# Gate and value projections of five feed-forward layers by seven products of block sums instead of eight, with the residual stream kept in DRAM between norms

## The chip, the cores and the metric

One core of a Trainium2 chip runs the whole network: two layers of a first block and one second block, 512 tokens of 1024 features, one launch. The metric is device time in microseconds. Names of the engines in the profile: PE is TensorE (matrix products), PEld its weight loads, DVE is VectorE, ACT is ScalarE, POOL is GpSimd, SP is SyncE, whose queue issues most DMAs. PSUM holds the results of TensorE in eight banks of 128x512 fp32; everything else lies in SBUF.

## The reference, cut to what matters

All arithmetic is fp32. The feed-forward layer occurs five times, twice in each layer of the first block and once in the second:

```python
D_MODEL, SEQ, D_FF = 1024, 512, 2816
def swiglu(x, w1, w3, w2):
    return (jax.nn.silu(x @ w1) * (x @ w3)) @ w2

for l in range(2):                                   # first block
    x = layer_norm(a * x + 0.5 * swiglu(x, ffn1...), ...)
    x = layer_norm(a * x + hybrid_mixer(x, ...), ...)
    x = layer_norm(a * x + 0.5 * swiglu(x, ffn2...), ...)
...                                                  # second block: recurrences, then
x = x + swiglu(rms_norm(x), ...)                     # its feed-forward, and a last rms_norm
```

## The kernel before, in words

**Exact products.** Activations lie feature-major: block k of 128 features is a tile of 128 partitions by 512 tokens (X0 to X7 for the residual stream). TensorE is fed with fp32r, a shortened fp32, so each operand is split in two: hi is the fp32r cast (ScalarE), lo is the operand minus hi (VectorE or POOL). One product is then three matrix products, hi with hi, hi with lo, lo with hi (`mm3`). In the trace x3h and x3l are the two parts of activation block 3, wraw a weight tile of 128x1024 as loaded, whi and wlo its parts (four buffers each; wraw has three), h0h to h21l the parts of the hidden blocks, kwh and kwl weight parts that are kept in slots.

**A feed-forward (`ffn`, line 714).** For each of 22 hidden blocks of 128 features the gate and the value are 8 blocks of x times a weight tile of 128x1024: 24 products of 512 columns in one PSUM bank (tile pu). ScalarE casts whi and applies SiLU to the gate (tile sl), VectorE makes wlo, multiplies by the value (sl<-sl,pu) and makes the low part of the hidden block; POOL has nothing to do there. The first three of the 44 banks are made together by `gemm_head`, 256 tokens at a time (72 products of 256 columns for each half), so that work can start while the norm before it is still on its second half. Then the down projection (`blocks`, tile po) makes 8 output blocks from 22 hidden blocks, the last two a half of the tokens at a time, and `layer_norm` adds each to X.

**A norm.** The last blocks of a projection come half by half, so the first half of the tokens is normed while TensorE makes the second. Statistics go through TensorE (sums, rbc: scale and offset spread to all partitions in PSUM), a chain of tiny VectorE operations (lnst), and then for each block VectorE multiplies and adds rbc, ScalarE writes the hi part, POOL the lo part.

**Order.** Each engine works through one fixed list. The lists are made when the kernel is recorded and do not always keep the order in which the code issues the work. Matrix weights are loaded by the SP queue in the order of use. All instructions pass through one wrapper, so that every row of the trace has the line L204; tiles and shapes tell them apart.

**Names that the steps touch:** `ffn` 714, `up` 710, `gemm_head` 459, `blocks` 444, `kept` 479, `wload` 395, `split` 409, `layer_norm` 592, `apply_norm` 649, `rms_end` 677, `start` and `first` at the end.

## Time and profile before

| | |
|---|---|
| three runs | 3388.19, 3385.47, 3387.38 us, median 3387.38 us |
| the profiled execution | span 3383.5 us from the first to the last instruction; the page gives no other time of its own, and the runs lie 2.0 to 4.7 us above it |
| granted TensorE clock, mean | 0.988 of full speed |
| busy | PE 97%, PEld 82%, DVE 51%, ACT 37%, POOL 17% |
| HBM | 274.76 MB read, 8.39 MB written, 84 GB/s over the span |

The chain of waits lies on TensorE for most of the span, and a good third of the span is the tile pu, the up-projections of the five feed-forwards. On POOL, 571.5 us are spread over the mixers, the norms and the second block. A matrix product's recorded duration is longer than the time to the next one's start, since they are pipelined: the pace is read from starts.

### The profile page before, as it was taken

How to read it: one execution, taken by the hardware profiler on the slowest of the kernel's cores; microseconds unless marked ns; L12 is line 12 of the kernel's file. 1: busy time of each engine (PE TensorE's matmuls, PEld its weight loads, DVE VectorE, ACT ScalarE, POOL GpSimd, SP SyncE). 2: the span in 40 equal slices, each digit the busy share in tenths (PEclk: the TensorE clock that was granted, in tenths of full speed). 3: DMA queues.
4: the chain of work that ended last, by engine and by line, in shares of the span. 5: the costliest groups of instructions: out<-in, count | busy, mean ns of one | idle time of the engine just before them, and what ended most of it. 6: DMA issues, size and time to landing. Idle time of an engine off the chain costs nothing.

```text
span 3383.5 us, 43373 instructions
## 1 busy us (share of the span) xinstructions
PE 3291.7 (97%) x17206; PEld 2759.6 (82%) x17210; DVE 1710.0 (51%) x3300; ACT 1242.4 (37%) x2224; POOL 571.5 (17%) x415
## 2 busy tenths in 40 slices
PE   9999999999999999999999999999999999999998
PEld 7888887788888888888778888888876777898887
DVE  4333668673333533366867433555526666443332
ACT  3232343543222422234354422335624444232221
POOL 0001430030002200044002100224442221030001
PEclk9999999999999999999899999989999999999999
DMA  4223211013233222322101223313341112423232
GB/s 157 97 93 108 63 58 57 7 51 100 95 94 105 82 95 97 98 72 70 57 7 51 85 96 96 109 56 104 116 130 64 61 65 88 145 88 100 94 97 72
DMA packets 88508, 285.96 MB, mean 85 GB/s; under 512 B 9840, under 2 KB 13552, under 8 KB 88304
## 3 DMA queue, kind: packets, MB, share of 16 engines
q1 hardware_dynamic: 83696, 275.84, 25.4%
q10 hardware_dynamic: 4608, 7.34, 0.7%
q8 instruction: 135, 2.21, 0.3%
q14 instruction: 69, 0.57, 0.1%
HBM read 274.76 MB, written 8.39 MB: 84 GB/s over the span
## 4 chain that ended last, share of the span: by engine, by line
PE 83%; DVE 9%; issue 3%; ACT 2%; POOL 2%; DMA 0%; SPq 0%; POOLq 0%; DVEq 0%; ACTq 0%
PE pu L204 35%; PE po L204 18%; PE sc L204 3%; PE pos L204 3%; PE pz L204 2%; PE pw L204 2%; PE so L204 2%; PE plx L204 2%; PE sz L204 2%; PE pgate L204 2%; PE pol L204 2%; POOL wlo L204 1%; PE ply L204 1%; PE pxb L204 1%; DVE isc L204 1%
## 5 line engine op out<-in xcount | busy, mean ns | idle before, releaser
L204 ACT CAST whi<-wraw 128x1024 fp32r<-128x1024 f32 (+7 forms) x507 | 507.9, 1003 | 1443.1 <-issue 486.0
L204 DVE TENSOR_TENSOR wlo<-wraw,whi 128x1024 fp32r<-128x1024 f32 (+1 forms) x326 | 394.0, 1209 | 613.9 <-ACT whi L204 598.9
L204 POOL TENSOR_TENSOR wlo<-wraw,whi 128x1024 fp32r<-128x1024 f32 (+6 forms) x181 | 394.1, 2181 | 630.4 <-ACT whi L204 622.7
L204 POOL TENSOR_TENSOR kwl<-wraw,kwh 128x512 fp32r<-128x512 f32 (+1 forms) x48 | 67.3, 1423 | 1694.6 <-ACT kwh L204 1677.2
L204 DVE TENSOR_TENSOR sl<-sl,pu 128x512 f32<-128x512 f32 x110 | 75.7, 688 | 343.8 <-PE pu L204 341.0
L204 PE MATMUL pu<-x0h,whi 128*128 128x512 f32 (+1 forms) x235 | 88.1, 379 | 7.1 <-ACT whi L204 7.1
L204 DVE SCALAR_TENSOR_TENSOR X<-X,po 128x512 f32<-128x512 f32 (+1 forms) x40 | 23.2, 580 | 138.8 <-PE po L204 138.8
L204 PE MATMUL pu<-x3l,whi 128*128 128x512 f32 (+1 forms) x235 | 88.4, 377 | 1.1 <-POOL x3l L204 1.1
L204 PE MATMUL pu<-x0l,whi 128*128 128x512 f32 (+1 forms) x235 | 88.6, 378 | 0.9 <-POOL x0l L204 0.9
L204 PE MATMUL pu<-x0h,wlo 128*128 128x512 f32 (+1 forms) x235 | 88.7, 378 | 0.6 <-DVE wlo L204 0.6
L204 PE MATMUL pu<-x1h,wlo 128*128 128x512 f32 (+1 forms) x235 | 88.7, 378 | 0.0
L204 PE MATMUL pu<-x2l,whi 128*128 128x512 f32 (+1 forms) x235 | 88.7, 378 | 0.0
L204 PE MATMUL pu<-x6l,whi 128*128 128x512 f32 (+1 forms) x235 | 88.2, 376 | 0.4 <-POOL x6l L204 0.4
L204 PE MATMUL pu<-x1l,whi 128*128 128x512 f32 (+1 forms) x235 | 88.6, 377 | 0.0
L204 PE MATMUL pu<-x4l,whi 128*128 128x512 f32 (+1 forms) x235 | 88.1, 376 | 0.4 <-POOL x4l L204 0.4
L204 PE MATMUL pu<-x5l,whi 128*128 128x512 f32 (+1 forms) x235 | 88.2, 376 | 0.2 <-POOL x5l L204 0.2
L204 ACT ACTIVATE sp<-sc,st 128x384 f32<-128x384 f32 (+3 forms) x128 | 66.6, 527 | 59.3 <-DVE st L204 47.0
L204 PE MATMUL pu<-x2h,wlo 128*128 128x512 f32 (+1 forms) x235 | 88.3, 377 | 0.0
L204 PE MATMUL pu<-x1h,whi 128*128 128x512 f32 (+1 forms) x235 | 88.3, 377 | 0.0
L204 PE MATMUL pu<-x3h,wlo 128*128 128x512 f32 (+1 forms) x235 | 88.3, 376 | 0.0
L204 PE MATMUL pu<-x7h,whi 128*128 128x512 f32 (+1 forms) x235 | 88.2, 375 | 0.0
L204 PE MATMUL pu<-x7l,whi 128*128 128x512 f32 (+1 forms) x235 | 88.2, 375 | 0.0
(1628 smaller groups left out, 9589.7 us busy)
## 6 DMA issues: line engine op xcount, KB each, us to landing
wraw<-in_ffn_in_dram SPq DMA_DIRECT2D x220, 512.0 KB, 3.8
wraw<-in_ffn_out_dram SPq DMA_DIRECT2D x80, 512.0 KB, 3.6
wraw<-in_ffn_out_dram SPq DMA_DIRECT2D x40, 384.0 KB, 3.1
wraw<-in_w_xbc_dram SPq DMA_DIRECT2D x24, 512.0 KB, 3.2
wraw<-in_wout_dram SPq DMA_DIRECT2D x16, 512.0 KB, 3.3
wraw<-in_w_gate_dram SPq DMA_DIRECT2D x16, 512.0 KB, 3.2
wraw<-in_w_z_dram SPq DMA_DIRECT2D x16, 512.0 KB, 3.2
wraw<-in_w_ossm_dram SPq DMA_DIRECT2D x16, 512.0 KB, 3.7
```

Of the source, the lines that this page charges most:

```text
L204: return f(*[_plain(x) for x in args], **{k: _plain(x) for k, x in kw.items()})
```

## The change

The hidden features are taken in 11 units of 256. A unit's gate and value weights are four quarters of 128x1024: a and b are the gate's for features 0 to 511 and 512 to 1023 of x, c and d the value's. x has four quarters as well, halves of the features by halves of the tokens. Seven products of sums of quarters replace the eight products of quarters (Strassen's form, in Winograd's arrangement); each is 24 matrix products of 256 columns, and results are added up in PSUM and by VectorE.

- `Unit` does a unit: it loads a, b, c, d (0.5 MB each, the same bytes as before), makes the sums s = c + d, s - a and b - (s - a) on VectorE and a - c on POOL, splits each of the seven weights (hi on ScalarE; lo on VectorE for products 1, 6 and 3, on POOL for 2, 5, 7 and 4), and puts the outputs together (su1, su5, su6 copied by ScalarE, three additions and four half multiplications on VectorE).
- `quarter_sums` makes t5, t6 (VectorE) and t7, t4 (POOL), sums of quarters of x, and splits them, once for each feed-forward, when the second half of the tokens has been normed.
- Hidden blocks (tiles hr) stay unsplit and are split later (hdh, hdl), by turns on VectorE and POOL, most of them during the last unit.
- To make room the residual stream is stored to DRAM after each norm (`spill`, SP's queue) and fetched again before the next down or output projection (`refill`, ScalarE's queue). 67 slots instead of 73; six wraw buffers instead of three. `blocks` keeps 16 of the 22 weight blocks of its first tail block and loads the other six for each half.

An up-projection was 984 matrix products of 512 columns and 144 of 256; it is now 1848 of 256 (11 units of 7 by 24). POOL's list grows from 420 to 782 rows.

```diff
-        for j in range(22):
-            pg, pu = (first.pop(0) if first else self.gemm(w, xs, "pu") for w in self.up(i, j))
-            s = self.a("sl")
-            nc.scalar.activation(s, pg, AF.Silu)
-            nc.vector.tensor_tensor(s, s, pu, op=OP.mult)
-            hid.append(self.split(s, f"h{j}"))
+        n = 11
+        plan = [(0, 1), (0, 2), (1, 1), (1, 2)] + [(0, p) for p in (5, 6, 3, 7)] + [(1, 5), (0, 4)] + [(1, p) for p in (6, 3, 7)]
+        for u in range(2, n):
+            plan += [(u, 1), (u, 5), (u, 2), (u - 1, 4), (u, 6), (u, 3), (u, 7)]
+        plan.append((n - 1, 4))
+        self.join_banks()
+        for u, p in plan:
+            if u not in units:
+                units[u] = Unit(self, io["ffn_in"][i, u], u < 2)
+            hidden = units[u].product(p, ops[p])
...
+            while raw and len(self.slots) > 8 + 2 * len(units) + 2 * (n - 1 - u):
+                hid.append(self.split(raw.pop(0), "hd", (nc.vector, nc.gpsimd)[len(hid) % 2]))
+        while raw:
+            hid.append(self.split(raw.pop(0), "hd", (nc.vector, nc.gpsimd)[len(hid) % 2]))
+        self.part_banks()
+        self.refill(x, home)
         yield from self.blocks([io["ffn_out"][i, m] for m in range(KD)], hid, "po", 2)

+class Unit:
+    def halves(self, raw, lower):
+        hi = net.wp.tile([P, WCH], F32R, name="whi", tag="whi", bufs=4)
+        lo = net.wp.tile([P, WCH], F32R, name="wlo", tag="wlo", bufs=4)
+        net.nc.scalar.copy(hi, raw)
+        lower.tensor_tensor(lo, raw, hi.bitcast(F32), op=OP.subtract)
...
+        if p == 5:
+            s = raw["s"] = net.wp.tile([P, WCH], F32, name="wraw", tag="wraw", bufs=6)
+            c, d, a = (self.load(q) for q in "cda")
+            dve.tensor_tensor(s, c, d, op=OP.add)
+            w = self.halves(s, pool)
+            pool.tensor_tensor(c, a, c, op=OP.subtract)
+            dve.tensor_tensor(s, s, a, op=OP.subtract)
+            return w
+        if p == 6:
+            return self.halves(raw["s"], dve)
+        if p == 3:
+            b = self.load("b")
+            dve.tensor_tensor(b, b, raw["s"], op=OP.subtract)
+            return self.halves(b, dve)
+        return self.halves(raw["c" if p == 7 else "d"], pool)
...
+        for f in range(2):
+            for k, (x, c) in enumerate(xs):
+                w = slice((4 * f + k) * P, (4 * f + k + 1) * P)
+                for j, (l, r) in enumerate(((hi, x[0]), (hi, x[1]), (lo, x[0]))):
+                    nc.tensor.matmul(bank[:, HALVES[f]], l[:, w], r[:, c], ...)
+        if p in (1, 5, 6):
+            s = sums[p] = net.a(f"su{p}")
+            nc.scalar.copy(s, bank)
+        elif p in (2, 3):
+            s = sums[{2: 1, 3: 6}[p]]
+            tt(s, bank, s, op=OP.add)
+            nc.scalar.activation(s, s, AF.Silu)
+        elif p == 7:
+            tt(sums[5], bank, sums[5], op=OP.add)
+            self.out = [net.a("hr") for _ in range(2)]
+            for o, h in zip(self.out, HALVES):
+                tt(o[:, HALVES[1]], sums[6][:, h], sums[5][:, h], op=OP.mult)
+        else:
+            for o, h in zip(self.out, HALVES):
+                tt(o[:, HALVES[0]], sums[1][:, h], bank[:, h], op=OP.mult)

+    def quarter_sums(self, ys, i, ops):
...
+            dve.tensor_tensor(t[5], a2, a1, op=OP.subtract)
+            dve.tensor_tensor(t[6], b2, t[5], op=OP.subtract)
+            pool.tensor_tensor(t[7], b2, a2, op=OP.subtract)
+            pool.tensor_tensor(t[4], b1, t[6], op=OP.subtract)
+        for n, lower in ((5, dve), (6, dve), (7, pool), (4, pool)):
+            q = self.split(ts.pop(n), f"t{n}", lower)
```

**VectorE, in the middle of an up-projection** (names: wlo, sl, h2l as above; su1, su5, su6 partial results, hr the unsplit hidden block, the numbers are buffers). Before, for one hidden block and the next:

```order
L204 TENSOR_TENSOR wlo<-wraw,whi 128x1024
L204 TENSOR_TENSOR h2l<-sl,h2h 128x512
L204 TENSOR_TENSOR wlo<-wraw,whi 128x1024
L204 TENSOR_TENSOR sl<-sl,pu 128x512
L204 TENSOR_TENSOR wlo<-wraw,whi 128x1024
L204 TENSOR_TENSOR h3l<-sl,h3h 128x512
```

and now, for one unit of two hidden blocks:

```order
L214 TENSOR_TENSOR wlo_1691<-wraw_1588,whi_1690 128x1024
L214 TENSOR_TENSOR wlo_1722<-wraw_1627,whi_1721 128x1024
L214 TENSOR_TENSOR wraw_1817<-wraw_1818,wraw_1820 128x1024
L214 TENSOR_TENSOR su1_1586<-pu_1633,su1_1586 128x512
L214 TENSOR_TENSOR hr_1551<-su1_1357,pu_1332 128x256
L214 TENSOR_TENSOR hr_1552<-su1_1357,pu_1332 128x256
L214 TENSOR_TENSOR wlo_1787<-wraw_1784,whi_1786 128x1024
L214 TENSOR_TENSOR wraw_1817<-wraw_1817,wraw_1784 128x1024
L214 TENSOR_TENSOR su6_1718<-pu_1600,su6_1718 128x512
L214 TENSOR_TENSOR wraw_1856<-wraw_1856,wraw_1817 128x1024
L214 TENSOR_TENSOR su5_1625<-pu_1561,su5_1625 128x512
L214 TENSOR_TENSOR hr_1780<-su6_1718,su5_1625 128x256
```

Three sums of weight tiles (wraw on both sides of the arrow) have joined three low parts (wlo); one half multiplication more, the second hr of products 7, follows.

**POOL, at the head of the second feed-forward, after the mixer's norm.** Before, the low parts of the first half of the tokens are followed by those of the second:

```order
L204 TENSOR_TENSOR x4l_6559<-X4_108,x4h_6558 128x256
L204 TENSOR_TENSOR x5l_6561<-X5_120,x5h_6560 128x256
L204 TENSOR_TENSOR x6l_6563<-X6_126,x6h_6562 128x256
L204 TENSOR_TENSOR x7l_6565<-X7_132,x7h_6564 128x256
L204 TENSOR_TENSOR x0l_6551<-X0_72,x0h_6550 128x256
```

and now:

```order
L214 TENSOR_TENSOR x4l_7683<-X4_7181,x4h_7682 128x256
L214 TENSOR_TENSOR wlo_7968<-wraw_7959,whi_7967 128x1024
L214 TENSOR_TENSOR x5l_7685<-X5_7183,x5h_7684 128x256
L214 TENSOR_TENSOR x7l_7689<-X7_7187,x7h_7688 128x256
L214 TENSOR_TENSOR x6l_7687<-X6_7185,x6h_7686 128x256
L214 TENSOR_TENSOR x4l_7683<-X4_7181,x4h_7682 128x256
L214 TENSOR_TENSOR t7_7748<-X4_7181,X0_7173 128x256
L214 TENSOR_TENSOR t4_7749<-X4_7181,t6_7747 128x256
L214 TENSOR_TENSOR x5l_7685<-X5_7183,x5h_7684 128x256
L214 TENSOR_TENSOR t7_7748<-X5_7183,X1_7175 128x256
L214 TENSOR_TENSOR t4_7749<-X5_7183,t6_7747 128x256
L214 TENSOR_TENSOR t7l_7767<-t7_7748,t7h_7766 128x512
```

A weight's low part (wlo_7968, that of product 5 of unit 0) has come between the first half's x4l and x5l, and the sums t7 and t4 with their splits between the second half's low parts.

**POOL, in the last unit of the first feed-forward** (hdl: low part of a hidden block). Before, POOL does nothing there. Now:

```order
L214 TENSOR_TENSOR wlo_2574<-wraw_2571,whi_2573 128x1024
L214 TENSOR_TENSOR wlo_2605<-wraw_2278,whi_2604 128x1024
L214 TENSOR_TENSOR hdl_2560<-hr_865,hdh_2559 128x512
L214 TENSOR_TENSOR hdl_2568<-hr_1094,hdh_2567 128x512
L214 TENSOR_TENSOR hdl_2669<-hr_1323,hdh_2668 128x512
L214 TENSOR_TENSOR hdl_2677<-hr_1552,hdh_2676 128x512
L214 TENSOR_TENSOR hdl_2732<-hr_2239,hdh_2731 128x512
L214 TENSOR_TENSOR wlo_2744<-wraw_2521,whi_2743 128x1024
```

Five low parts of hidden blocks stand between those of the weights of product 4 of the unit before and of product 7 of the last unit (wlo_2744).

## Rows read from the trace of the kernel before

**Rows 1.** The profile page, parts 1 and 4: busy times, the chain that ended last.
```profile
PE 3291.7 (97%) x17206; PEld 2759.6 (82%) x17210; DVE 1710.0 (51%) x3300; ACT 1242.4 (37%) x2224; POOL 571.5 (17%) x415
...
PE 83%; DVE 9%; issue 3%; ACT 2%; POOL 2%; DMA 0%; SPq 0%; POOLq 0%; DVEq 0%; ACTq 0%
PE pu L204 35%; PE po L204 18%; PE sc L204 3%; PE pos L204 3%; PE pz L204 2%; PE pw L204 2%; PE so L204 2%; PE plx L204 2%; PE sz L204 2%; PE pgate L204 2%; PE pol L204 2%; POOL wlo L204 1%; PE ply L204 1%; PE pxb L204 1%; DVE isc L204 1%
```

**Rows 2.** Windows of the five up-projection stages: span, then busy time of each engine.
```profile
28.57:251.80 223.23, 223.23 (x987) 184.91 (x986) 79.27 (x85) 68.05 (x88) 0.00 (x0) 1.00 0.31 101
746.37:991.99 245.62, 243.86 (x1147) 204.27 (x1146) 96.76 (x137) 81.36 (x111) 11.17 (x15) 1.00 0.28 91
1120.37:1363.06 242.69, 242.61 (x1145) 203.97 (x1145) 91.36 (x124) 75.60 (x102) 7.63 (x11) 1.00 0.28 93
1858.97:2104.26 245.29, 243.66 (x1147) 204.27 (x1147) 95.84 (x138) 81.36 (x110) 11.11 (x15) 1.00 0.28 92
3007.26:3249.20 241.94, 241.67 (x1138) 203.01 (x1137) 85.12 (x106) 72.57 (x97) 5.73 (x9) 1.00 0.29 93
```

**Rows 3.** Timeline, TensorE, at 100 us: start, duration, instruction; first and seventh of a run.
```profile
99.77 0.39 PE L204 MATMUL pu<-x0h,wlo 128*128 128x512 f32 x1
...
101.13 0.39 PE L204 MATMUL pu<-x2h,wlo 128*128 128x512 f32 x1
```

**Rows 4.** Timeline, TensorE, at 350 us: first and ninth of a run of 256 columns.
```profile
349.79 0.28 PE L204 MATMUL po<-h20l,kwh 128*128 128x256 f32 x1
...
350.75 0.28 PE L204 MATMUL po<-h1h,whi 128*128 128x256 f32 x1
```

**Rows 5.** Groups by shape, ScalarE and VectorE: count, busy us, mean ns, idle before.
```profile
L204 ACT CAST whi<-wraw 128x1024 fp32r<-128x1024 f32 x413 | 434.5, 1053 | 1211.1 <-issue 461.0 <-PE pu L204 395.7 <-PE po L204 153.4
L204 ACT ACTIVATE sl<-pu 128x512 f32<-128x512 f32 x110 | 64.2, 589 | 0.0
...
L204 DVE TENSOR_TENSOR wlo<-wraw,whi 128x1024 fp32r<-128x1024 f32 x296 | 365.4, 1235 | 503.3 <-ACT whi L204 488.4
...
L204 DVE TENSOR_TENSOR sl<-sl,pu 128x512 f32<-128x512 f32 x110 | 75.7, 688 | 343.8 <-PE pu L204 341.0 <-ACT sl L204 2.7
```

**Rows 6.** Timeline at the head of the second feed-forward: POOL and VectorE.
```profile
756.21 0.73 POOL L204 TENSOR_TENSOR x7l<-X,x7h 128x256 fp32r<-128x256 f32 x1
...
757.76 1.67 DVE L204 TENSOR_TENSOR X<-X,rbc 128x256 f32<-128x256 f32 x4 [0.80 <-PE rbc L204]
...
766.48 0.73 POOL L204 TENSOR_TENSOR x7l<-X,x7h 128x256 fp32r<-128x256 f32 x1 [0.19 <-ACT X L204]
```

**Rows 7.** Timeline (us), POOL and VectorE, where VectorE reads PSUM (ply).
```profile
2307.48 2.40 POOL L204 TENSOR_TENSOR wlo<-wraw,whi 128x1024 fp32r<-128x1024 f32 x1 [2.85 <-ACT whi L204]
...
2307.93 0.69 DVE L204 SCALAR_TENSOR_TENSOR lq<-lq,ply 128x512 f32<-128x512 f32 x1 [2.15 <-ACT lq L204]
```

**Rows 8.** Tile kwl on POOL: duration ns min/median/max.
```profile
L204 POOL TENSOR_TENSOR kwl<-wraw,kwh x48: 730/1299/2270, 318.5 to 3325.2; 128x512 fp32r<-128x512 f32 x43, 128x256 fp32r<-128x256 f32 x5
```

**Rows 9.** The profile page, part 6: weight loads, KB each, median us to landing.
```profile
wraw<-in_ffn_in_dram SPq DMA_DIRECT2D x220, 512.0 KB, 3.8
```

**Rows 10.** Timeline, POOL and VectorE, where VectorE reads two tiles of SBUF.
```profile
2302.23 2.41 POOL L204 TENSOR_TENSOR wlo<-wraw,whi 128x1024 fp32r<-128x1024 f32 x1 [1.46 <-ACT whi L204]
...
2302.91 2.27 DVE L204 TENSOR_TENSOR li<-li,lu 128x512 f32<-128x512 f32 x1
...
318.54 3.83 POOL L204 TENSOR_TENSOR kwl<-wraw,kwh 128x512 fp32r<-128x512 f32 x2 [318.02 <-ACT kwh L204]
...
319.44 1.78 DVE L204 TENSOR_TENSOR wlo<-wraw,whi 128x1024 fp32r<-128x1024 f32 x1 [0.46 <-ACT whi L204]
```

**Rows 11.** Timeline at the start, VectorE and ScalarE: constants landed, fourth weight tile landed.
```profile
16.92 0.63 DVE L204 CAST bfc<-cst 128x128 bf16<-128x128 f32 x4 [0.69 <-DMA cst<-in_cst_dram]
...
18.19 1.05 ACT L204 CAST whi<-wraw 128x1024 fp32r<-128x1024 f32 x1 [3.49 <-DMA wraw<-in_ffn_in_dram]
```

**Rows 12.** Timeline at the head of the fifth feed-forward, VectorE.
```profile
3012.39 3.22 DVE L204 SCALAR_TENSOR_TENSOR rn<-xr,vec,rbc 128x256 f32<-128x256 f32 x8 [0.87 <-PE rbc L204]
```

More of the change, by code (lines that the diff above doesn't have):

```diff
@@ L490, in kept @@
                 self.nc.gpsimd.tensor_tensor(lo[:, :w], r, hi[:, :w].bitcast(F32), op=OP.subtract)
-                out += [[q[:, i * P:(i + 1) * P] for q in (hi, lo)] for i in range(w // P)]
+                out += [[q[:, i * P:(i + 1) * P] for q in (hi, lo)] + [(hi, lo)] for i in range(w // P)]
         return out
@@ L644, in layer_norm, with order, apply_norm @@
         xs = self.operands()
+        ops = self.quarters(xs) if feed else None
         while halves:
-            self.apply_norm(x, xs, halves.pop(0), g, b, then)
-        return xs
-    def apply_norm(self, x, xs, half, g, b, then):
+            self.apply_norm(x, xs, halves.pop(0), g, b, then, ops)
+        return ops or xs
+    def order(self, c, ops):
+        return (0, 4, 1, 5, 2, 6, 3, 7) if ops and c.start else range(KD)
+    def apply_norm(self, x, xs, half, g, b, then, ops):
         nc = self.nc
         c, rm, q = half
-        for k in range(KD):
+        for k in self.order(c, ops):
             y = x[k][:, c]
@@ L680, in rms_end @@
         n = c.stop - c.start
-        for k in range(KD):
-            self.scaled_operand(x[k][:, c], self.v(w, k), rp[:, :n], *(o[:, c] for o in xs[k]))
+        for k in self.order(c, ops):
+            y = ys[k][:, c]
+            nc.vector.scalar_tensor_tensor(y, x[k][:, c], self.v(w, k), rp[:, :n], op0=OP.mult, op1=OP.mult)
+            if k >= 4 or not c.start:
+                h, l = (o[:, c] for o in xs[k])
+                nc.scalar.copy(h, y)
+                nc.gpsimd.tensor_tensor(l, y, h.bitcast(F32), op=OP.subtract)
+            if c.start and k in (5, 7):
+                self.quarter_sums(ys, k // 2 - 2, ops)
     def rms_norm(self, blocks, x, scale, w, out=None):
@@ L687, in rms_norm @@
         q = self.running("qs")
-        xs, left = [], {0: KD, 256: KD}
+        ops, left = None, {0: KD, 256: KD}
         for m, c, p in blocks:
@@ L697, in rms_norm @@
             if out is None:
-                xs = xs or self.operands()
-                self.rms_end(x, xs, q[0], w, c)
+                if not ops:
+                    xs, ys = self.operands(), [self.a("rn") for _ in range(KD)]
+                    ops = self.quarters(xs)
+                    self.rms_end(x, xs, ys, ops, q[0], w, c)
                 continue
@@ L1563, in second @@
         x = [self.fetch(dx, k, f"xr{k}") for k in range(KD)]
-        xs = self.rms_norm(self.blocks([io["w_o2"][m] for m in range(KD)], o, "po2", 4), x, 0.5, "norm2_w")
+        ops = self.rms_norm(self.blocks([io["w_o2"][m] for m in range(KD)], o, "po2", 4), x, 0.5, "norm2_w")
         o.clear()
-        self.rms_norm(self.ffn(4, xs), x, 1.0, "norm_f_w", out=io["out"])
+        home = self.spill(x, "dy")
+        self.rms_norm(self.ffn(4, ops, x, home), x, 1.0, "norm_f_w", out=io["out"])
     def start(self):
-        x, xs, head = [], [], []
-        srcs = self.up(0, 0) + self.up(0, 1)[:1]
+        x, xs = [], []
+        units = {u: Unit(self, self.io["ffn_in"][0, u], True) for u in range(2)}
         for k in range(KD):
```

138 lines of the change are left out of this document (109 added, 29 removed).

## The prediction

> **What bounds the kernel now.** I read the page first, then the five up-projections by windows, then single instructions. TensorE is busy 97% of the span and carries 83% of the chain; the tile pu alone is 35% of it [rows 1]. In the five windows TensorE is busy nearly throughout and is granted a clock of 1.00, its 2.4 GHz level, while VectorE works 79 to 97 us of some 240, ScalarE 68 to 81, POOL almost nothing [rows 2]. So an up-projection lasts as long as its matrix products, and the change takes products away. What it gives them to (VectorE, POOL) has time on average; whether it has it at the right moments decides the rest.
>
> **What goes.** Six starts of 512 columns span 1.36 us, 0.2267 each [rows 3]; eight of 256 columns span 0.96 us, 0.120 each [rows 4]. An up-projection was 984 x 0.2267 + 144 x 0.120 = 240.4 us of pure products; now 1848 x 0.120 = 221.8. That is 18.6 us for each, **93 us for five**. An eighth of the columns goes, but the smaller products cost 7 ns more for each 256 columns, so 7.7% is left.
>
> The Trainium skill ("TensorE: Matmul & The Clock Gate", section "Wait — 56ns, not 53.3ns?") gives start-to-start times of N columns at 2.4 GHz plus about 2.5 ns, so 109 and 216 ns; by that the gain would be some 130 us. This kernel's products take 13 ns over the columns [rows 3, 4], and the measurement decides.
>
> **What a unit asks of the other engines.** A unit lasts 168 x 0.120 = 20.16 us on TensorE.
> - ScalarE: 7 casts of a weight at 1.05, and 7 operations of 512 columns (3 copies, 2 SiLU, 2 hidden blocks) at 0.59 [rows 5]: 11.5 us.
> - VectorE: 6 operations of 1024 (three low parts, three sums) at 1.24, 3 additions of 512 at 0.69 [rows 5], 4 multiplications of 256 at 0.42 [rows 6], one hidden block at 0.69: 11.9 us.
> - POOL: 5 operations of 1024 at 2.40 [rows 7], and one hidden block at 1.30 [rows 8] in the units that split one: 12.0 to 13.3 us.
> - DMA: four loads of 0.5 MB, each 3.8 us from issue to landing [rows 9], with six buffers instead of three: the same 2 MB as before in 20.16 us instead of 21.8.
>
> Each is below 20.16. But VectorE and POOL don't run side by side freely. A VectorE operation that reads PSUM takes its 0.69 us beside a POOL low part of 2.40 [rows 7]. One that reads two tiles of SBUF doesn't: li<-li,lu of 512 columns took 2.27 us and ended only when POOL's 2.41 were over; and two kwl of 1.30 took 3.83 instead of 2.60 beside a wlo, which itself took 1.78 [rows 8, 10]. The 1.23 us that POOL lost is all of the wlo. They exclude each other, by turns.
>
> So I add up what reads two tiles of SBUF: on VectorE the 6 x 1.24 and the two multiplications of product 7 at 0.42, 8.3 us; on POOL 12.0. Together **20.3 us of a unit's 20.16**. The shared path is just full, and over it by 2 us in a unit that splits hidden blocks. Is TensorE late at once? The weights of a product can be made from the end of the product four before it, 8.6 us ahead; hi needs 1.05, lo at most 2.40 + 1.24 of waiting, so about 4 us are spare. Walking a unit through both lists, each low part is ready 4 us or more early; a drift of 0.2 us for each of 11 units stays within that. I take nothing for the units (bounds 0 and 11 us a feed-forward, one us for each unit).
>
> [...] If both engines ran at their own pace, as their averages in rows 2 would let one think, POOL would need 12 us of 20 and nothing below would have its upper bound.
>
> **What is added around the units.** Five places, each with a bound without exclusion and one with.
> - *Start of the first feed-forward.* The constants land by 16.9 us and the fourth weight tile at 18.2, a tile each 1.3 us [rows 11]. The queue now has one tile fewer ahead of the constants, so tiles a and b of unit 1 land at about 17 and 18, and c, d, a of unit 0 at 19.5 to 22: product 5 can't be prepared before. X4 lands at 9.5 (2.4 MB come between it and the constants' end at 15.6, at that pace). From there POOL's list has twelve quarter sums and splits and a low part (13.5 us), the low part of product 2 of unit 1 (2.4), a - c (2.4) and product 5's own (2.4): ready at 30 us, or 38 if VectorE's operations on two SBUF tiles, some 8 us, come between. TensorE has 96 products, 11.5 us, until then: 18.7 to 26.5 lost. Before, it was 28.6 us for 17.3 of products: 11.3. So +7 to +15; I take 12.
> - *Heads after the mixers (second and fourth feed-forward).* Before, 5.2 and 4.9 us are lost there (245.62 and 245.29 against 240.4) [rows 2]: x7l of the first half ends at 756.9, the second half's first block is written from 757.8, its last low part ends at 767.2 [rows 6]. Now POOL's wlo of product 5 comes before x5l (+2.4), VectorE waits for it (s - a stands inside the chain of lnst): the second half starts 3 us later, at 761. From there to the second t5l VectorE has 16 operations on rbc, 7 quarter sums, 5 splits or adds of 512, 3 of 1024: 15 us, or 21 with POOL's turns. t5l at 776 to 782, for 116 products, 13.9 us, since 746.4: 16 to 22 lost, and 3 more where product 7's weights wait behind POOL's last t4l. So +10 to +20, I take 14 each, 28.
> - *Head of the third*, with a two-block tail ahead and weight loads on SP behind the spill: 2.3 lost before [rows 2]; the same list, less of it: +5 to +14, I take 9.
> - *Head of the fifth.* The eight rn take 3.22 us [rows 12], 1.5 lost before [rows 2]; quarter sums as above: +3 to +10, I take 7.
> - *Two mixers' entries.* The x operands and the residual's loads wait for slots: 0 to 8, I take 4.
>
> **End of each feed-forward.** Product 4 waits for the su5 addition in its own bank: 0.7 us. And 17 hidden blocks are split in the last unit: POOL's five hdl ahead of product 7's low part, VectorE's two ahead of product 6's and two more ahead of product 3's. By turns (8 x 1.30 and 9 x 0.69, 16.6 us more on the shared path, against sums for a next unit that fall away) product 6 comes 1 us late, 7 one, 4 two; if ScalarE's casts keep up with all, up to 6. I take 3, five times: 15 (bounds 4 and 30).
>
> **The sum.** 12 + 28 + 9 + 7 + 4 + 15 = 75 us against 93: 18 us faster. The profiled span of 3383.5 becomes 3365; the median of the runs lies 3.9 above that span, so **3369 us** (own range 3350 to 3383).
>
> **Rivals.**
> - *The places cost little more than now.* For it: VectorE's li that waited is one of few such rows, and both engines are half idle [rows 1]. Lower bounds: 7 + 20 + 5 + 3 + 0 + 4 = 39, so 3387 - 54 = 3333.
> - *POOL is late (slower).* It is one mechanism: POOL's list, with VectorE's turns between, becomes what TensorE waits for at each head and each end. Upper bounds: 15 + 40 + 14 + 10 + 8 + 30 = 117, 24 us slower, 3411; it decides from 93 us on. For it: rows 10, and that the shared path is full in each unit. If the units are late too, 0.5 us each for 55, 3439. Against it: 4 us spare for each weight.
> - *No change:* gains and losses meet, 86 to 100 us, 3380 to 3394.
> - *The products don't keep 0.120 us.* The same shapes with new weights each time keep it in the tail of a down projection [rows 4], so little speaks for it; at 0.130 it would cost 92 us.
>
> **How the numbers follow.** Forecast 0.40, little cost 0.15, late POOL 0.33 (units late too 0.08 of it), no change 0.11, products 0.01. A run tells 0.2%, 7 us, from nothing. Faster: 0.40 less the part of its range above 3380 (0.02), and 0.15: 0.53. Same: 0.11 and 0.02: 0.13. Slower: 0.33 and 0.01: 0.34. The range holds 8 in 10 with the lower half of the cheap case and the units' delay left out: 3332 to 3420.
>
> **What would show it.** In the profile after: pu products 0.120 us apart in the middle of a feed-forward, each up-projection's middle units 20.2 us (right) or above 21 with PE waiting for POOL wlo (late POOL); POOL's low parts of 1024 at 2.5 to 3.6 us instead of 2.40, VectorE's sums above 1.24; PE waits at pu for DVE t5l and POOL wlo at the second and fourth head of 15 to 25 us; some 3 us of waits for wlo and su5 in each last unit. I am wrong in the main if the units themselves are longer than 20.5 us, or if the heads cost under 5 us.

## The result: 6.4% slower, and the profile after

The changed kernel takes **3605.3 us** (median; 3604.3 to 3606.5) where the kernel before takes 3387.5. The ratio is 1.0643 (95% interval 1.063 to 1.0655). I had said 3369, with a range up to 3420: wrong in sign and far outside the range.

The page of the changed kernel, parts 1 and 4, beside [rows 1]:
```profile
PE 3303.5 (92%) x20806; PEld 2942.7 (82%) x20810; DVE 2284.9 (63%) x3696; ACT 1496.4 (42%) x2584; POOL 1376.3 (38%) x777
...
PE 61%; DVE 16%; issue 7%; ACT 6%; POOL 6%; DMA 4%; ACTq 0%; DVEq 0%; POOLq 0%; SPq 0%
PE po L214 17%; PE pu L214 16%; POOL wlo L214 3%; DMA wraw<-in_ffn_in_dram 3%; DVE wraw L214 3%; PE pos L214 2%; ACT whi L214 2%; PE pz L214 2%; PE sc L214 2%; PE so L214 2%; PE pw L214 2%; PE pgate L214 2%; PE plx L214 2%; PE pol L214 2%; PE sz L214 1%
```
TensorE's share of the chain fell from 83 to 61%, pu's from 35 to 16%. VectorE, "issue", ScalarE, POOL and DMA took that place. POOL's busy time went from 572 to 1376 us, still only 38% of the span.

The five up-projections by windows (first to last product; columns as in [rows 2]), then the second one cut into its head, middle and end:
```profile
6.68:286.20 279.52, 242.65 (x1848) 237.56 (x1849) 196.34 (x178) 126.48 (x170) 166.44 (x77) 0.93 0.36 116
794.28:1077.79 283.51, 242.98 (x1865) 237.31 (x1865) 198.65 (x206) 129.78 (x179) 167.30 (x83) 0.92 0.31 97
1208.69:1489.07 280.38, 240.04 (x1857) 235.28 (x1858) 196.09 (x196) 126.48 (x173) 170.23 (x84) 0.94 0.32 100
2002.95:2279.69 276.74, 240.12 (x1857) 235.56 (x1858) 194.27 (x198) 128.81 (x175) 165.81 (x82) 0.94 0.32 99
3195.05:3470.14 275.09, 241.93 (x1863) 237.77 (x1862) 195.33 (x183) 121.59 (x166) 163.37 (x80) 0.93 0.30 95
...
794.28:841.00 46.72, 29.88 (x187) 27.62 (x188) 34.30 (x63) 24.44 (x40) 32.21 (x26) 0.74 0.23 74
841.00:1017.00 176.00, 164.69 (x1345) 162.97 (x1344) 122.85 (x105) 74.63 (x95) 100.05 (x40) 0.99 0.32 98
1017.00:1077.79 60.79, 48.41 (x339) 46.73 (x337) 41.50 (x39) 30.71 (x44) 35.04 (x18) 0.86 0.38 113
```
An up-projection should have come down from 240 to 222 us of products, and came up to 275 to 284. VectorE's and POOL's busy times together make 363 us of 280 in the first, where before they made 79 to 108 of some 240. Where TensorE waits most, the granted clock is 0.74 and 0.86 (its two levels are 1.2 and 2.4 GHz, so part of such a window ran at the lower), where before it was 1.00 [rows 2]. That is a second loss on top of the waits.

The products themselves are what I took them for. Timeline, TensorE, the first and eleventh product of a run of 256 columns in a middle unit (beside [rows 4]):
```profile
99.78 0.28 PE L214 MATMUL pu<-x6l,whi 128*128 128x256 f32 x1
...
100.97 0.28 PE L214 MATMUL pu<-x5h,wlo 128*128 128x256 f32 x1
```
Ten steps take 1.19 us, 0.119 each.

Now one period of a middle unit, VectorE's timeline, then POOL's, then of ScalarE's and TensorE's the rows that the reading needs: start, duration, instruction, and in brackets the idle time before it and what ended it (beside [rows 10]):
```profile
129.30 1.23 DVE L214 TENSOR_TENSOR wraw<-wraw 128x1024 f32<-128x1024 f32 x1 [3.83 <-DMA wraw<-in_ffn_in_dram]
130.44 0.68 DVE L214 TENSOR_TENSOR su<-pu,su 128x512 f32<-128x512 f32 x1
131.04 0.74 DVE L214 TENSOR_TENSOR hr<-su,pu 128x256 f32<-128x256 f32 x2
132.76 1.38 DVE L214 TENSOR_TENSOR wlo<-wraw,whi 128x1024 fp32r<-128x1024 f32 x1 [0.98 <-ACT whi L214]
136.43 3.41 DVE L214 TENSOR_TENSOR wraw<-wraw 128x1024 f32<-128x1024 f32 x1 [2.29 <-POOL wlo L214]
139.76 0.68 DVE L214 TENSOR_TENSOR su<-pu,su 128x512 f32<-128x512 f32 x1
140.36 1.21 DVE L214 TENSOR_TENSOR wraw<-wraw 128x1024 f32<-128x1024 f32 x1
141.50 0.68 DVE L214 TENSOR_TENSOR su<-pu,su 128x512 f32<-128x512 f32 x1
142.28 2.87 DVE L214 TENSOR_TENSOR hr<-su,su 128x256 f32<-128x256 f32 x2
145.08 1.21 DVE L214 TENSOR_TENSOR wlo<-wraw,whi 128x1024 fp32r<-128x1024 f32 x1
...
130.66 2.40 POOL L214 TENSOR_TENSOR wraw<-wraw 128x1024 f32<-128x1024 f32 x1 [2.93 <-DVE wraw L214]
133.75 5.01 POOL L214 TENSOR_TENSOR wlo<-wraw,whi 128x1024 fp32r<-128x1024 f32 x2 [0.69 <-ACT whi L214]
142.12 2.41 POOL L214 TENSOR_TENSOR wlo<-wraw,whi 128x1024 fp32r<-128x1024 f32 x1 [3.37 <-ACT whi L214]
...
131.16 0.63 ACT L214 ACTIVATE su<-su 128x512 f32<-128x512 f32 x1 [6.46 <-DVE su L214]
131.70 1.97 ACT L214 CAST whi<-wraw 128x1024 fp32r<-128x1024 f32 x2
133.58 0.58 ACT L214 COPY su<-pu 128x512 f32<-128x512 f32 x1
...
134.21 0.39 PE L214 MATMUL pu<-t7h,whi 128*128 128x256 f32 x1 [1.90 <-ACT su L214]
```
At 129.3 s = c + d. At 133.75 POOL starts on s's low part (product 5). At 136.43 VectorE may overwrite s with s - a, after 2.29 us of waiting, because POOL had to be done reading s. By then POOL has begun its next low part, and s - a takes 3.41 us instead of 1.23. The pair hr<-su,su takes 2.87 us, beside POOL's low part at 142.12 (0.75 in e5 below, where POOL is idle). What is queued behind on VectorE comes as much later. The su additions and hr<-su,pu, which read PSUM, keep 0.68 and 0.74 for two. The unit's period here is 22.0 us instead of 20.16.

How this reaches TensorE the last rows show. TensorE stops once in this period, 1.90 us ahead of product 7, for ScalarE's copy of product 6's result. That copy stands behind two casts and a SiLU, and the SiLU had waited for VectorE's addition at 130.44, which stands behind s = c + d. This sum had itself waited 3.83 us for a load, and a load waits until one of the six wraw buffers is free: from 76 to 230 us SP's queue waited 67.5 us for VectorE's sums, 53.2 for POOL's low parts and 15.6 for VectorE's. From s, ScalarE's cast and POOL's low part lead to s - a, and what stands behind s - a on VectorE leads to the next free buffer and load: a loop through four queues. Over the whole kernel TensorE waits at pu mostly for ScalarE (in all, times, longest):
```profile
PE pu L214 <- ACT su L214: 83.1, 38, 4.0
...
PE pu L214 <- DVE su L214: 27.3, 12, 4.7
```
My sign for a late POOL, TensorE waiting at pu for POOL's wlo, makes 10.9 us in 8 waits: POOL's lateness arrives under other engines' names.

From the starts of the pu products I made this balance of the profiled executions (168 starts are a unit; pure units and before's own 16.8 us of losses taken off):

| us against before | I said | changed | e15 | e5 | e13 |
|---|---|---|---|---|---|
| products taken away | -93 | -93.2 | -93.2 | -93.2 | -93.2 |
| first two units of each, with the start's part | +56 | +110.6 | +98.4 | +78.7 | +66.9 |
| units 3 to 9 | 0 | +70.3 | +18.1 | +0.9 | +2.5 |
| last two units | +15 | +88.1 | +66.8 | +25.6 | +25.3 |
| between the up-projections | +4 | +44.3 | +40.2 | +24.3 | +13.0 |
| sum | -18 | +220.1 | +130.3 | +36.3 | +14.5 |

The spans differ by 220.1 (3603.6 against 3383.5). The last three columns are experiments told below.

### The profile page after: what moved, and what is told of

The parts are those of the page before. It is cut to its first block, busy times and chain, and to the rows that moved or that the text cites. A ratio compares the mean times of both kernels' runs of the same rounds, so it can differ in the third digit from the quotient of the medians.

```text
span 3603.6 us, 52432 instructions
## 1 busy us (share of the span) xinstructions
PE 3303.5 (92%) x20806; PEld 2942.7 (82%) x20810; DVE 2284.9 (63%) x3696; ACT 1496.4 (42%) x2584; POOL 1376.3 (38%) x777
## 3 DMA queue, kind: packets, MB, share of 16 engines
q1 hardware_dynamic: 94208, 300.88, 26.8%
## 4 chain that ended last, share of the span: by engine, by line
PE 61%; DVE 16%; issue 7%; ACT 6%; POOL 6%; DMA 4%; ACTq 0%; DVEq 0%; POOLq 0%; SPq 0%
PE po L214 17%; PE pu L214 16%; POOL wlo L214 3%; DMA wraw<-in_ffn_in_dram 3%; DVE wraw L214 3%; PE pos L214 2%; ACT whi L214 2%; PE pz L214 2%; PE sc L214 2%; PE so L214 2%; PE pw L214 2%; PE pgate L214 2%; PE plx L214 2%; PE pol L214 2%; PE sz L214 1%
## 5 line engine op out<-in xcount | busy, mean ns | idle before, releaser
L214 POOL TENSOR_TENSOR wlo<-wraw,whi 128x1024 fp32r<-128x1024 f32 (+5 forms) x399 | 930.3, 2337 | 1106.6 <-ACT whi L214 1106.3
L214 ACT CAST whi<-wraw 128x1024 fp32r<-128x1024 f32 (+5 forms) x682 | 679.2, 1006 | 861.6 <-PE po L214 348.6
L214 DVE TENSOR_TENSOR wraw<-wraw 128x1024 f32<-128x1024 f32 x165 | 323.0, 1957 | 293.1 <-POOL wlo L214 151.4
L214 PE MATMUL po<-hdl,whi 128*128 128x512 f32 (+1 forms) x940 | 340.4, 362 | 0.0
L214 PE MATMUL po<-hdh,whi 128*128 128x512 f32 (+1 forms) x940 | 338.2, 360 | 0.0
L214 PE MATMUL po<-hdh,wlo 128*128 128x512 f32 (+1 forms) x940 | 338.1, 360 | 0.0
L214 PE MATMUL pu<-t7h,whi 128*128 128x256 f32 x440 | 139.7, 317 | 83.2 <-ACT su L214 83.1
L214 PEld LDWEIGHTS po<-hdh,wlo 128*128 128x128 f32 x940 | 179.7, 191 | 26.7 <-issue 1.0
L214 PEld LDWEIGHTS po<-hdl,whi 128*128 128x128 f32 x940 | 179.8, 191 | 26.4 <-issue 1.0
L214 PEld LDWEIGHTS po<-hdh,whi 128*128 128x128 f32 x940 | 179.9, 191 | 25.4
```

The costliest lines, as they stand in the source:

```text
L214: return f(*[_plain(x) for x in args], **{k: _plain(x) for k, x in kw.items()})
```

## Experiments

Theory A: the ring of six weight buffers closes a loop. B: GpSimd's low parts hold VectorE up, by exclusion and by being waited for. C: late hidden splits. D: quarter sums in the heads. Times are medians; the changed kernel is 3605.

**e1_sum_buffer.** The sum s leaves the ring.
```diff
-            s = raw["s"] = net.wp.tile([P, WCH], F32, name="wraw", tag="wraw", bufs=6)
+            s = raw["s"] = net.wp.tile([P, WCH], F32, name="wsum", tag="wsum", bufs=1)
-NSLOT = 67
+NSLOT = 65
-        few = min(16, len(xs))
+        few = min(8, len(xs))
```


> The changed kernel with the sum s = c + d in a buffer of its own, so that the ring of six holds only loads; two arena slots fewer pay for it, and the down-projection's second-to-last block keeps 8 of its 22 weight blocks instead of 16 and loads the rest twice. Theory A (the ring closes a loop: c of a unit can be loaded only when s of the unit before is split, which gives 22.0 us a unit instead of 20.16): units 3 to 9 fall from 22.0 to 20.2-20.8, 5 x 7 x 1.4 = 50 us and some of the last two units, time 3535 to 3560. Theory B (VectorE and GpSimd shut each other out of SBUF, so that a unit needs 22 us of exclusive port time whatever the buffers): units stay at 21.6-22, time 3590 to 3606. Theory C (the losses sit at heads and ends, where hidden splits and quarter sums are): within 10 us of 3605.

Measured: 3595.3 (ratio to before 1.0611, 1.0582 to 1.0639). Units 3 to 9 stay at 22.1 us on average. Theory A as it is put here falls: it is not the place that s takes in the ring. Loads wait for buffers in e1 as well (from 76 to 230 us SP's queue waited 60.3 us for POOL's low parts, 43.9 for VectorE's and 38.3 for its sums), so a loop that passes through the loads isn't excluded by this run.

**e2_hidden_high.** The hidden blocks' low parts are not made.
```diff
-                hid.append(self.split(raw.pop(0), "hd", (nc.vector, nc.gpsimd)[len(hid) % 2]))
+                hid.append(self.high_only(raw.pop(0)))
```


> The changed kernel without the low parts of the hidden blocks: the high part stands in for the low one in the down-projection, the slots are still taken, every product is still run. Theory C (seventeen splits that come in the last unit of each up-projection cost what the last two units lose, 88 us over five, and part of what follows): 3605 - 50 to -80, time 3525 to 3555, last two units at 20.2-23 instead of 26-31. Theory A (the ring): the last units wait for c and d too, so they stay above 25 and the time is 3585 to 3600; the middle units stay at 22.0 under A, since no hidden block is split there beyond two a unit.

Measured: 3551.2. The last two units fall from 57.9 to 46.6 us on average, the middle stays at 22.4. So C is a part of the ends, 57 us, and of nothing else.

**e3_pool_high.** GpSimd's four low parts of a unit are not made.
```diff
+        if lower is net.nc.gpsimd:
+            return hi, hi
         lower.tensor_tensor(lo, raw, hi.bitcast(F32), op=OP.subtract)
```


> The changed kernel without the low parts of the weights of products 2, 5, 7 and 4, which GpSimd makes: the high part stands in for them, products unchanged. It takes 4 x 2.34 us a unit off GpSimd. Theory B (exclusive port) and theory A (the ring's loop, in which s - a waits for GpSimd's subtraction: 3.41 instead of 1.23 us, and hr 2.54 instead of 0.41) both bring the middle units to 20.2-20.6: 3605 - 65; B also frees heads and ends, where GpSimd is the busiest engine: -60 to -120 more, time 3420 to 3480. A alone, with heads and ends unchanged: 3535 to 3550.

Measured: 3389.7. Each unit from the second to the tenth runs at 20.2 us, in all five; the last two take 41.2, the pure time and 0.9, with all late splits in place. Theory B: 216 us hang on these 220 subtractions, about as much as the 218 that the change lost. The 93 us of products taken away are still not won: in this run the first two units cost 66 us and the stretches between the up-projections 32. It does not say yet how the subtractions cost, by exclusion or by waiting.

**e4_no_quarter_sums.** The operands of one block stand in for the sums.
```diff
     def quarter_sums(self, ys, i, ops):
+        self.plain_operands(ys, i, ops)
+        return
```


> The changed kernel without the quarter sums and their splits: the operands of one block stand in for those of products 5, 6, 7 and 4, the slots are still taken, every product is still run. Theory D (the heads, +22 us each against before, wait for the sums on GpSimd and for the clock that falls meanwhile): the first two units go from 65-69 us to 42-48, 5 x 15 to 20 = 75 to 100 off, time 3505 to 3530. Rival (the heads wait for x low parts and for the weights' splits, which stay): less than 8 us a head, time 3565 to 3605.

Measured: 3545.4. The first two units fall from 65.8 to 55.4 us on average: the sums are 10 us a head, less than D said, and 15 of the 25 us lost there hang on other things. The last two units come down by 4 us as well, and the middle units go up to 22.7, for which this run gives no reason.

**e5_vector_lows.** A whole version: all work on the units' weights on VectorE.
```diff
-            w = self.halves(s, pool)
-            pool.tensor_tensor(c, a, c, op=OP.subtract)
+            w = self.halves(s, dve)
             dve.tensor_tensor(s, s, a, op=OP.subtract)
+            dve.tensor_tensor(c, a, c, op=OP.subtract)
-        return self.halves(raw["c" if p == 7 else "d"], pool)
+        return self.halves(raw["c" if p == 7 else "d"], dve)
```
and likewise for product 2.


> The changed kernel with all work on the weights of the up-projections on VectorE: the low parts of products 2, 5, 7 and 4 and the difference a - c too; GpSimd keeps the head's and the hidden blocks' share. Nothing is left out. Theory B (what GpSimd subtracts out of SBUF stops VectorE and comes late itself): VectorE's queue of some 18 us a unit, without the lock (7 x 1.23 low parts, 4 x 1.23 sums, 3 x 0.69, 4 x 0.41, half a hidden split), still fits into 20.16, middle units at 20.2-20.8, ends at 41-46 for two units, time 3395 to 3440. Rival E (VectorE becomes the bound, its queue is in order and its waits for loads and ScalarE's casts add up): middle units 21.3-23, time 3470 to 3570.

Measured: 3422.9 (1.0109, 1.0094 to 1.0124), 182 us less than the changed kernel by moving work to the engine that was the busier. Middle units 20.16 (20.28 in the third up-projection). The same 22 us by windows, of the changed kernel and then of e5:
```profile
118.00:140.00 22.00, 20.10 (x168) 19.90 (x167) 14.80 (x14) 9.43 (x12) 12.77 (x5) 1.00 0.31 96
```
```profile
118.00:140.00 22.00, 22.00 (x186) 22.00 (x185) 18.15 (x23) 11.32 (x14) 0.00 (x0) 1.00 0.37 119
```
With VectorE busy 18.15 us and POOL idle TensorE never waits; with 14.80 and 12.77 it does.

**e7_vector_high.** VectorE's low parts (products 1, 6, 3) are not made.
```diff
+        if lower is net.nc.vector:
+            return hi, hi
```


> The changed kernel without the low parts of products 1, 6 and 3, which VectorE makes (high part in their place); GpSimd's four stay. It takes 3 x 1.33 us a unit off VectorE and nothing off GpSimd. Theory B as mutual exclusion (time in which only one of the two gets at SBUF decides): middle units to 20.2-20.7, time 3500 to 3545. Rival F (GpSimd's subtractions are simply too slow and in order, 2.34 us each behind ScalarE's casts, and whoever needs them waits): middle units stay 21.5-22, time 3575 to 3605.

Measured: 3586.3; middle units 22.2 to 23.2. Pure exclusion falls: half of VectorE's instructions on weights are gone and the units are no shorter. VectorE's group of weight sums, of the changed kernel and then of e7 (count, busy, mean ns, idle before and what ended it):
```profile
L214 DVE TENSOR_TENSOR wraw<-wraw 128x1024 f32<-128x1024 f32 x165 | 323.0, 1957 | 293.1 <-POOL wlo L214 151.4 <-DMA wraw<-in_ffn_in_dram 139.1 <-issue 2.3
```
```profile
L214 DVE TENSOR_TENSOR wraw<-wraw 128x1024 f32<-128x1024 f32 x165 | 317.8, 1926 | 602.5 <-POOL wlo L214 430.1 <-DMA wraw<-in_ffn_in_dram 162.8 <-ACT whi L214 9.4
```
The time that VectorE gained it spends waiting for POOL's low part: 430 us instead of 151.

**e9_idle_pool.** e5, and GpSimd subtracts constants in each unit, for nobody.
```diff
+            scr = net.wp.tile([P, WCH], F32, name="wscr", tag="wscr", bufs=1)
+            pool.tensor_tensor(scr[:, :1], hi[:, :1].bitcast(F32), hi[:, :1].bitcast(F32), op=OP.subtract)
+            pool.tensor_tensor(scr, c[:, :WCH], c[:, NCST - WCH:], op=OP.subtract)
```


> e5 with four GpSimd subtractions of 128x1024 out of SBUF in every unit whose result nobody reads (each behind a 128x1 one that reads the product's high part, for the time of it), two arena slots fewer and 8 kept weight blocks as in the run with the sum's own buffer. Theory B as mutual exclusion: 9.4 us of GpSimd and some 15 us of VectorE with two SBUF inputs don't fit into 20.16 together, middle units 23 to 25.5, 55 x 3 to 5 above e5, time 3560 to 3700. Rival F (only a low part that is waited for costs anything): within 20 us of e5.

Measured: 3783.7 (1.1171), 361 us above e5, middle units 25.9 to 26.8. Nobody waits for these results (only ScalarE's casts, 6.0 us in all, until the small subtractions had read whi), and the slots and kept blocks given up, which the cut leaves out, cost nothing to be seen in e1. So this is exclusion, with the waits and the lower clock (0.942 of full speed against e5's 0.971) that follow from it. VectorE's groups of the units, of e5 and then of e9:
```profile
L214 DVE TENSOR_TENSOR wlo<-wraw,whi 128x1024 fp32r<-128x1024 f32 x473 | 596.1, 1265 | 185.8 <-ACT whi L214 184.6 <-issue 0.2
L214 DVE TENSOR_TENSOR wraw<-wraw 128x1024 f32<-128x1024 f32 x220 | 273.1, 1242 | 79.1 <-DMA wraw<-in_ffn_in_dram 75.6
L214 DVE TENSOR_TENSOR su<-pu,su 128x512 f32<-128x512 f32 x165 | 112.3, 683 | 2.3 <-PE pu L214 2.2
L214 DVE TENSOR_TENSOR hr<-su,su 128x256 f32<-128x256 f32 x110 | 47.2, 470 | 0.6
```
```profile
L214 DVE TENSOR_TENSOR wlo<-wraw,whi 128x1024 fp32r<-128x1024 f32 x473 | 826.6, 1760 | 121.3 <-ACT whi L214 120.8
L214 DVE TENSOR_TENSOR wraw<-wraw 128x1024 f32<-128x1024 f32 x220 | 334.6, 1521 | 125.3 <-DMA wraw<-in_ffn_in_dram 115.0 <-issue 6.5
L214 DVE TENSOR_TENSOR su<-pu,su 128x512 f32<-128x512 f32 x165 | 112.5, 682 | 1.4 <-PE pu L214 1.3
L214 DVE TENSOR_TENSOR hr<-su,su 128x256 f32<-128x256 f32 x110 | 82.6, 790 | 0.6
```
What reads two SBUF tiles grows by 39, 22 and 68% (327 us over these groups); what reads PSUM stays at 682 ns. The Trainium skill ("SBUF — State Buffer", section "Who interferes with whom") states that a VectorE instruction with at most one SBUF input, outside the two-port modes, doesn't contend with GpSimd; this trace agrees, 683 and 682 ns for su<-pu,su.

**e15_fifth_vector.** The changed kernel with one low part moved.
```diff
-            w = self.halves(s, pool)
+            w = self.halves(s, dve)
```


> The changed kernel with a single low part moved, that of product 5, from GpSimd to VectorE; those of 2, 7 and 4 and the difference a - c stay on GpSimd. Nothing is left out. It takes one dependency away (s - a waited for GpSimd's reading of s, 2.3 us in the unit at 118 to 140) and 2.3 of 11.7 us of GpSimd a unit. Waiting as the larger part (a chain that runs through GpSimd once a unit): middle units fall from 22.0 to 20.2-20.8, time 3605 - 60 to -110. Exclusion as the larger part (GpSimd still holds SBUF 9.4 us a unit against VectorE's 14 to 15): middle units 21.2-21.8, time 3605 - 10 to -45.

Measured: 3522.9 (1.0395, 1.0381 to 1.041), 82 us less. The middle units fall to 20.2 to 20.5 us in four of the five up-projections (22.2 in the fifth, and why stays open), with 9.4 of GpSimd's 11.7 us a unit still there. So in the middle the larger part hangs on the wait of s - a: all of VectorE's waits for POOL's low parts in this group fall from 151 to 70 us. e15 alone doesn't separate this from a shared path that is less full, since the sum of two-input times falls too, from 20.3 to 19.1 us. e7 does: there the sum is 16.6 us, the wait stays, and the units are no shorter. The lock itself is still in the rows: VectorE's groups of weights, of the changed kernel, and then of e15:
```profile
L214 DVE TENSOR_TENSOR wlo<-wraw,whi 128x1024 fp32r<-128x1024 f32 x253 | 344.8, 1375 | 155.9 <-ACT whi L214 153.3 <-issue 1.7 <-PE pu L214 0.7
```
```profile
L214 DVE TENSOR_TENSOR wlo<-wraw,whi 128x1024 fp32r<-128x1024 f32 x308 | 417.3, 1372 | 172.9 <-ACT whi L214 169.6 <-issue 2.1
L214 DVE TENSOR_TENSOR wraw<-wraw 128x1024 f32<-128x1024 f32 x165 | 320.5, 1943 | 191.2 <-DMA wraw<-in_ffn_in_dram 114.3 <-POOL wlo L214 69.9 <-issue 5.0
```
Means of 1372 and 1943 are as in the changed kernel. Heads and ends keep most of their loss (98 and 67 us).

**e8_three_ahead.** e5, and one more unit's products 1 and 2 ahead of the quarter sums.
```diff
-        plan = [(0, 1), (0, 2), (1, 1), (1, 2)] + ...
+        plan = [(u, p) for u in range(3) for p in (1, 2)] + ...
```
and the plan behind it without these two products.


> e5 with the products 1 and 2 of the third unit, too, ahead of the first product that needs a quarter sum: 48 more matrix products (5.8 us) beside the quarter sums of each head, for one more pair of loads. Nothing is left out. Theory D (what is left of the heads' loss is the wait for quarter sums on VectorE and GpSimd): 3 to 5.5 us less a head, 15 to 28 below e5. Rival: the sums are late because of VectorE's queue, which now holds two more low parts ahead of them: 0 to 10 above e5.

Measured: 3408.7 (1.007, 1.0055 to 1.0085): 14 below e5, just under what D said.

**e10_forward_free.** e8 with slots given back in the order of use.
```diff
                 del out
+        xs.reverse()
         xs.clear()
```


> e8 with one line more: the slots of a projection's operand blocks are given back in the order in which TensorE is done with them, where the list's clearing gave them back from the last to the first, so that x0h of the next stage takes the slot of a block that TensorE has read long before the end. Nothing is left out. Theory G (the entries of the two mixers and of the second part come 4.4, 6.3 and 11 us later than before because ScalarE's x0h waits for the last products of the projection): three entries x 4 to 7 us and two heads x 2 to 4, time 3408 - 15 to -28, 3380 to 3394. Rival (they are late because the refill and spill share queues and VectorE with the norm): within 5 us of e8.

Measured: 3404.5, 4 below e8: the rival's answer. But x0h still came last there, in the slot of the norm's last square, so theory G was tried only in part.

**e11_earlier_splits** and **e12_four_ahead.**
```diff
-            while raw and len(self.slots) > 8 + 2 * len(units) + 2 * (n - 1 - u):
+            while raw and len(self.slots) > 3 + 2 * len(units) + 2 * (n - 1 - u):
```
and for e12 `range(4)` in the plan above.


> e10 with five fewer slots held in reserve before a hidden block is split, so that some five of the seventeen late splits move out of the last unit. Nothing is left out. Theory C (what is left of the ends, 27 us over five, is VectorE's and ScalarE's queue full of late splits): last units from 24.5 to 22-23, 8 to 12 us below e10. Rival: the arena has then no free slot ahead and the sums su wait for slots: 0 to 15 above e10.

> e11 with the products 1 and 2 of a fourth unit ahead of the first quarter sum. Nothing is left out. Theory D: another 2 to 4 us a head, 10 to 20 below e11. Rival: the cover is enough already and what is waited for is VectorE's own queue, which gets two low parts more: 0 to 8 above e11.

Measured: 3403.7 and 3401.9. Neither differs measurably from e10, so neither C nor D gives what it said; the last units take 25.5 us in e11 and 24.3 in e10.

**e13_old_slots** (on e11) and **e16_after_slots** (on the changed kernel, with e10's line): one slot is held back.
```diff
+        last = self.a("last")
         xs = self.operands()
+        del last
```


> e11 with one slot held while the norm takes the slots of its operands, so that x0h does not take the slot that was given back last before them: that of the last square, which VectorE reads only behind the last product of the projection (x0h at 1498.6 in e11's trace, x1h at 1484.9). Nothing is left out. Theory G2 (what is left of the entries, zd 4 to 9 us late, is x0h's wait for that slot): x0h comes ahead of x1h, each of the three entries behind an up-projection gets back 3 to 7 us, time 3403 - 10 to -20, 3383 to 3394, about level with the kernel before. Rival (x0h is then early but TensorE waits for VectorE's sums of the norm all the same): within 4 us of e11.

> The changed kernel with the two edits on slots alone (operand blocks given back first to last; one slot held while the norm takes its own), the up-projections as they are. Nothing is left out. Theory G (of the 45 us that the stretches between up-projections lose against before, the entries behind up-projections are slots that TensorE still reads): the stretches come down by 10 to 25 us together, time 3580 to 3595. Rival: the entries wait for GpSimd's low parts of x and of the kept weights, which stay: within 5 us of 3605.

Measured: 3402.1 (1.0043, 1.003 to 1.0055) and 3598.9 (1.0624). ScalarE at the second mixer's entry, of e11 and then of e13:
```profile
1484.91 0.60 ACT L214 ACTIVATE x1h<-X,vec 128x256 fp32r<-128x256 f32 x1
...
1498.55 0.60 ACT L214 ACTIVATE x0h<-X,vec 128x256 fp32r<-128x256 f32 x1 [0.49 <-DVE qs L214]
```
```profile
1484.00 0.60 ACT L214 ACTIVATE x0h<-X,vec 128x256 fp32r<-128x256 f32 x1
1484.50 0.59 ACT L214 ACTIVATE x1h<-X,vec 128x256 fp32r<-128x256 f32 x1
```
The mechanism is shown: x0h comes 14 us earlier, and the first products of the two mixers' entries, counted from the end of the up-projection, are 0.8 us ahead of before and 0.7 behind it, where in e11 they were 3.6 and 8.5 behind. The time of e13 is hardly less (1.5 us): at the next waits of the mixer most of it is given back. In e16's profiled execution the stretches between the up-projections are 14 us shorter (30 instead of 44), of which its median shows 6.4, between what the two theories said.

**e14_head_pool** (on e13): product 2's low parts of the units ahead on GpSimd.
```diff
-            return self.halves(self.load("b", not self.ahead), dve)
+            return self.halves(self.load("b", not self.ahead), pool if self.ahead else dve)
```


> e13 with the low parts of product 2 of the three units that run ahead in each head on GpSimd instead of VectorE, 13 to 14 low parts in all; in the middle everything stays on VectorE. Nothing is left out. Theory D2 (what is left of the heads is VectorE's queue: TensorE waits up to 6.3 us for a low part that stands behind the norm there): 1 to 4 us less a head, 5 to 18 below e13. Rival B (GpSimd has its own queue of low parts and sums in the head, and each of its subtractions stops VectorE): 0 to 15 above e13.

Measured: 3407.0, 5 above e13, and the intervals of the two overlap (1.0043 to 1.0068, 1.003 to 1.0055). Theory D2's 5 to 18 us less don't come; that the head got longer isn't shown.

**e17_splits_behind** (on e13) and **e18_scale_on_scalar** (on e17).
```diff
-            while raw and len(self.slots) > 3 + 2 * len(units) + 2 * (n - 1 - u):
+            while raw and u < n - 1 and len(self.slots) > 3 + 2 * len(units) + 2 * (n - 1 - u):
...
-                if k % 2:
+                if k % 2 or ops:
```


> e13 with no hidden block split during the last unit: its thirteen or so splits come behind the weights of the last product, beside the down-projection's first block, which needs one operand block per 0.7 us. Nothing is left out. Theory C2 (the last unit's 5 us over 20.2, 26 over five, are splits that stand ahead of the weights in VectorE's queue, each longer while GpSimd subtracts): last units 20.2-22, 3402 - 12 to -25, 3377 to 3390, level with or just below the kernel before. Rival (the down-projection's first block then waits for its operands): the same 3 to 6 us a time come back behind the last product, 3398 to 3412.

> e17 with the four even blocks' scale and bias of each fed norm's halves on ScalarE instead of VectorE, some 1.6 us less on VectorE in three heads. Nothing is left out. Theory D3 (the heads' 16 us each are VectorE's queue): 2 to 6 below e17. Rival (ScalarE's casts come later by 0.6 us each instead): within 4 us of e17 or above.

Measured: 3403.5 and 3407.0. Theory C2 falls: the last units get longer, 27.0 us on average instead of 25.2. Of D3's 2 to 6 us nothing comes: e18 is 3.5 us above e17. No version beats the kernel before; the best are within half a per cent above it.

## Why the prediction was wrong, step by step

- **"93 us for five"**: right. The products keep 0.119 us, and e3's and e5's units run at 20.16.
- **"I take nothing for the units"**: the step that failed first, +70 us. I found the shared path just full (20.3 of 20.16 us), and then argued it away: "each low part is ready 4 us or more early". That walk treated every low part by itself. But VectorE's queue is in order, and in it stands an instruction, s - a, that overwrites what POOL is still reading. It waits for ScalarE's cast and POOL's 2.4 us, then for POOL's next hold of SBUF (2.29 and 2.18 us in the unit shown), and everything behind it waits too: the additions, ScalarE's SiLU and copies after them, and the buffers for the next loads. TensorE meets it as a wait for ScalarE's su. e15 takes that one dependency away, with 2.3 us of GpSimd's work, and the middle falls to 18 us of loss; e7 leaves the dependency and shortens VectorE, and nothing falls. I had named this very wait for the heads ("VectorE waits for it") and not for the 35 middle units.
- **"They exclude each other, by turns"**: right, and cheap only on paper. I used it as a sum of busy times. By e9 671 us of idle GpSimd subtractions (and 171 of small ones) cost 361 us where VectorE is busy 17 us of a unit (18.15 of 22). Whether a path that is full by a sum of means would have been enough to make the units late without the wait of s - a, no run separates: at 19.1 us of 20.16 (e15) most units keep their time, at 16.6 with the wait (e7) they don't. By the same sum e9, where nobody waits for POOL's results, asks for 24 us, and its units take 26.
- **"Heads" and "Start"**: 56 said, 111 measured. With GpSimd out of the units' weights 79 are left; the quarter sums alone were some 50 (e4). I had 15 to 25 us of waits for t5l and POOL's wlo in the second head; there were 17, for t5h and X above all (6.0 us each). On top comes the clock, 0.74 there, which I had at nothing: the 187 products keep TensorE busy for 29.9 us, and at 0.120 each would take 22.4.
- **"End of each feed-forward"**, 3 us each: 17.6 measured. My walk had the right splits in the right queues; e2 shows that they cost 57 of 88 us, and e3 that without POOL's weights the same splits cost 0.9 us each time. The price was that of both together.
- **"Two mixers' entries"**, 4 us: 44 between the up-projections. I had named the wait for slots; e13 shows it at each entry behind an up-projection, but its repair gives back little. With GpSimd out of the units 24 are left. How the rest divides among the refills, the norms' tails and the heads' order isn't settled.
- **The bounds.** "Late POOL" with late units was among the rivals, at 3439 and 0.08. Its 0.5 us for each unit was half of a bound that I had set by feeling; measured are 2.0 in the middle. That rival is the one that came, and it was 166 us short. And I added five bounds as if they were independent, where one cause (GpSimd's low parts) moved all of them: in e3 they go together, 216 us.

## What to carry to other kernels

When work is handed to two engines that share a path to SBUF, add up their instructions with two SBUF inputs. Where the sum came to 20.3 us of a 20.16 us period here, the units took 22.0, and giving all of the weights' work to one engine was better: e5 put more on the busier one and won 182 us. Before calling a wait covered, look in each in-order queue for the instruction that overwrites or frees what another engine reads, and count all that stands behind it. In this kernel 7.7% less time for matrix products didn't pay even with the middle units at their pure time (e5): the heads, the ends and the stretches between, where little covers the added vector work, took more than it gave.
